# A fp32 hybrid encoder step: gated tiles stored from the gate's tile, and five pieces of work moved in the order

## The chip, the cores and the metric

One core of one Trainium2 chip. The metric is the device time of one execution in microseconds (us), taken as the median of the runs. Five engines work side by side: TensorE (PE) multiplies, VectorE (DVE), ScalarE (ACT) and GpSimd (POOL) work element by element, and SyncE (SP) issues loads and stores. POOL can issue transfers too, among them one that adds what it loads to what is already there. Each engine runs its instructions in a fixed order and waits where an operand or a buffer isn't ready yet.

## The reference, cut to what matters

One step of a two-layer streaming encoder, width 2048, over 512 new frames of one stream and 64 frames of another: 576 columns, which the kernel treats as two halves of 288. Everything is fp32.

```python
h = rmsnorm(x, g0)                                   # layer 0: gated linear attention
q, k, v, r, a1 = split(h @ w_in)
loga = log_sigmoid(a1 @ w_a2 + b_a) / 16             # per head: decay, summed over time
o = recurrence(q, k, v, loga, state)                 # 4 heads, key 256, value 512
o = o * rsqrt(mean(o * o) + eps) * g_norm
x = x + (o * silu(r)) @ w_out
h = rmsnorm(x, g1)                                   # layer 1: convolution module
a, ga, z = split(h @ w_in1 + b_in)
c = depthwise_conv31(a * sigmoid(ga), state) + b
c = silu(layernorm(c)) * silu(z)
y = rmsnorm(x + c @ w_out1, g_final)
```

## The kernel before

**Matmuls.** Each fp32 product is made of three: high part by high part (L225), high by low (L228), low by high (L231; in the stages with sums of blocks all three are on L394). Weights come in chunks of 512 KB. For each chunk SP loads `raw` (L117), ACT copies it to the high part `whi` (L125), and the low part `wlo` comes either from a DVE subtraction (L127) or, for the chunk numbers in `dma_lo` (L605), from an ACT copy with the sign turned (L129) and an adding transfer that POOL issues (L130). There are two `raw` buffers and four of `whi` and `wlo`. In the sum stages `raw` blocks are also subtracted from each other (L185), and sums of the activations are made and split (L1107, L1108, L1116 to L1119).

**Stages**, in us from the span's start. To 62: x is loaded, its squares are summed for the norm (ACT L690, POOL and DVE L691, last sum L712), the gate's low-rank product psA (L702) and the first group of q run on TensorE; the second gate weight `wa2r` is split into `w2s` by two DVE casts and a subtraction (L728 to L730) and stored to `w2d`, from where each head loads it later. To 440: the projections. 440 to 700: the heads. 700 to 930: the output projection of layer 0. 930 to 1500: the input projection of the convolution module, with the depthwise convolution on DVE, POOL and ACT; the layer norm's centring (L1313), squares (L691, L1319), mean square on TensorE (m_c L540, from ACT's high part ssch L544 and DVE's low part) and inverse root (L562 to L566) lie at 1360 to 1402, and `finish` (DVE L1324, ACT L1325, POOL L1326) then gates each of the 16 channel blocks. 1500 to 1690: the output projection, whose first pair of blocks takes the seven-product form.

**Heads.** For head h the program issues: attention, gates of head h-1 (`rblk`), decay of head h+1 (`decay`), `output(h)`, scores, states, norm. `output` writes the 512 prompt columns (ACT L974) and the 64 sample columns (DVE copy L981) of four value tiles into `ob`, of which there is one buffer (`big`). `rblk` multiplies each value tile by its gate on POOL (L1022), in place in `ob`, and SP stores it to `spill` (L1024). `decay` forms pz on TensorE (L861, L863), takes ACT functions of it (L865 to L867), and sums it over time on DVE: L868, ten scans (L873), small terms (L880 to L889) and L895; the k and q tiles are then scaled by it (L903). Temporary tiles of 128 x 576, gates, squares and loads among them, share a ring of six (`s2`, made by `tmp`).

**Order.** A scheduler orders each engine's instructions from the program's order and its own estimates; `tc.high_priority` lets an instruction pass others, and `tc.issue_after(x)` keeps it behind x in that order.

Of the kernel before, what the change touches and what calls it, by code (L numbers as in the profile page):

```python
# [17 lines left out]
P = 128  # L18
# [31 lines left out]
def emit(nc, tc, x, wg, wa1, wa2, wgo, wc, wco, par, s0, y, sp_out, ss_out, cv_out):  # L50
# [127 lines left out]
    def plan_full(w1, w2, ra):  # L178


        d = {}

        def diff(out, a, b):
            with tc.high_priority(offset=PRIO):
                nc.vector.tensor_tensor(out, a, b, ALU.subtract)  # L185

        def u0(i):
            d["r1"] = load_raw(w1, 0, f"raw{i}", *wx[ra])
            to_unit(i, d["r1"])

        def u1(i):
            d["r2"] = load_raw(w2, 0, f"raw{i}")
            diff(d["r1"], d["r2"], d["r1"])
            to_unit(i, d["r1"])

        def u2(i):
            d["r3"] = load_raw(w2, 1, f"raw{i}", *wx["r3"])
            diff(d["r2"], d["r3"], d["r2"])
            diff(d["r1"], d["r3"], d["r1"])
            to_unit(i, d["r1"])  # L200

        def u4(i):
            d["r4"] = load_raw(w1, 1, f"raw{i}")
            to_unit(i, d["r4"])

        def u5(i):
            diff(d["r1"], d["r4"], d["r1"])
            to_unit(i, d["r1"])

        chunks.extend([u0, u1, u2, lambda i: to_unit(i, d["r2"]), u4, u5,  # L210
                       lambda i: to_unit(i, d["r3"])])

# [9 lines left out]
    def mm_k(ps, hi, lo, kk, k):  # L222
        st, sp = k == 0, k == KT - 1
        for j in range(2):
            nc.tensor.matmul(ps[j], hi[:, kk, :], ah[k][:, j * HT : (j + 1) * HT],  # L225
                             start=st, stop=False)
        for j in range(2):
            nc.tensor.matmul(ps[j], hi[:, kk, :], al[k][:, j * HT : (j + 1) * HT],  # L228
                             start=False, stop=False)
        for j in range(2):  # L230
            nc.tensor.matmul(ps[j], lo[:, kk, :], ah[k][:, j * HT : (j + 1) * HT],  # L231
                             start=False, stop=sp)

    def mm_chunk(ps, ci, half):
        hi, lo = ready.pop(ci)
# [366 lines left out]
    base_c = len(chunks)  # L602
    plan(conv_groups, lambda b: wc[b])
    base_co = len(chunks)
    dma_lo.update(range(4, base_p), range(base_l + 3, base_o + 4), range(base_c + 4, base_co + 4))  # L605
    plan([[0, 1]], lambda f: wco[f])
    for f in range(2, 14, 2):
        plan_full(wco[f], wco[f + 1], ("rb", "ra")[f // 2 % 2])
# [100 lines left out]
    for k in range(KT):  # L709
        with tc.issue_after(split15) if k >= SQ_EARLY else nullcontext():  # L710
            add_sq(sqs[k // 8], xk(k)[:, 0, :], k % 8 == 0, f"x{k}", nc.gpsimd if k < 8 else nc.vector)
    nc.vector.tensor_tensor(ssq, ssq, sqs[1], ALU.add)  # L712
    a3f = s2.tile([96, T], F32, tag="s2", name="a3f")
    a3 = page(10, [96, T], "a3s", F32R)
    for j in range(2):
# [9 lines left out]
        nc.sync.dma_start(wa2r, wa2)  # L725
        nc.sync.dma_start(pr[:, PC_A:], par[:, PC_A:])
    w2 = page(9, [96, 1024], "w2s", F32R)
    nc.vector.tensor_copy(w2[:64], wa2r[:64])  # L728
    nc.vector.tensor_copy(w2[64:], wa2r[64:])
    nc.vector.tensor_tensor(w2[64:], wa2r[64:], w2[64:].bitcast(F32), ALU.subtract)  # L730
    nc.sync.dma_start(w2d, w2.bitcast(F32))

    rstd0 = rstd_from([parts(ssq, "ssx")], float(D), "x")
# [118 lines left out]
    def decay(h):  # L852
        d = hd[h]
        a3, w2 = d["aw"]
        c2 = gp.tile([P, 2, T], F32, tag="qk", name=f"c2_{h}", bufs=3)
        eq = gp.tile([P, 2, T], F32, tag="qk", name=f"eq{h}", bufs=3)
        for dt in range(2):
            f = 2 * h + dt
            for j in range(2):
                pz = px.tile([P, 512], F32, tag="ms", bufs=2, name=f"pz{f}_{j}")  # L860
                nc.tensor.matmul(pz[:, :HT], w2[:96, dt * P : (dt + 1) * P], a3[:96, j * HT : (j + 1) * HT],  # L861
                                 start=True, stop=True)
                nc.vector.tensor_scalar(eq[:, dt, j * HT : (j + 1) * HT], pz[:, :HT], col(PC_BA, f), -1.0,  # L863
                                        ALU.add, ALU.mult)
        nc.scalar.activation(c2, eq, AF.Abs)  # L865
        nc.scalar.activation(c2, c2, AF.Exp, scale=-1.0)
        nc.scalar.activation(c2, c2, AF.Ln, bias=1.0)  # L867
        nc.vector.scalar_tensor_tensor(eq, eq, 0.0, c2, ALU.max, ALU.add)  # L868
        for dt in range(2):
            for i in range(5):  # L870
                n = P if i < 4 else TS
                ts = slice(i * P, i * P + n)
                nc.vector.tensor_tensor_scan(c2[:, dt, ts], ones[:, :n], eq[:, dt, ts], 0.0, ALU.mult, ALU.add)  # L873
        sm = gp.tile([P, 2, 13], F32, tag="sm", name=f"sm{h}")
        ke = gp.tile([P, 2, 11], F32, tag="ke", name=f"ke{h}", bufs=2)
        km, ee = ke[:, :, :5], ke[:, :, 5:]
        r = sm[:, :, 0:4]
        tt = sm[:, :, 4:8]
        m = sm[:, :, 8:13]
        nc.vector.tensor_copy(r, c2[:, :, 63:TP:P])  # L880
        nc.vector.tensor_copy(tt, c2[:, :, 127:TP:P])
        for i in (2, 1, 0):
            nc.vector.tensor_tensor(tt[:, :, i : i + 1], tt[:, :, i : i + 1], tt[:, :, i + 1 : i + 2], ALU.add)
        nc.vector.tensor_tensor(m[:, :, 0:4], r, tt, ALU.subtract)
        nc.vector.tensor_scalar(m[:, :, 4:5], c2[:, :, T - 1 : T], -1.0, None, ALU.mult)
        nc.scalar.activation(km, m, AF.Exp, scale=1.0 / GN)
        o = 0
        for i in range(3):
            nc.vector.tensor_tensor(ee[:, :, o : o + 3 - i], m[:, :, i + 1 : 4],  # L889
                                    m[:, :, i : i + 1].broadcast_to([P, 2, 3 - i]), ALU.subtract)  # L890
            o += 3 - i
        nc.scalar.activation(ee, ee, AF.Exp, scale=-1.0 / GN)
        for dt in range(2):
            cv = c2[:, dt, :TP].rearrange("p (i t) -> p i t", i=4)
            nc.vector.tensor_tensor(cv, cv, r[:, dt, :].unsqueeze(2).broadcast_to([P, 4, P]), ALU.subtract)  # L895
        nc.scalar.activation(eq, c2, AF.Exp, scale=-1.0 / GN)
        nc.scalar.activation(c2, c2, AF.Exp, scale=1.0 / GN)
        d.update(eq=eq, ek=c2, km=km, ee=ee)
# [60 lines left out]
    def output(h):  # L959
# [7 lines left out]
        for vt in range(4):  # L967
            vc = slice(vt * P, vt * P + P)
            po = px.tile([P, 512], F32, tag="main", bufs=2, name=f"po{h}{vt}")
            for i in range(4):  # L970
                for n, (a, b) in enumerate(pairs):
                    nc.tensor.matmul(po[:, i * P : TP], a[:, i, vc], b[:, OFFS[i] : OFFS[i] + TP - i * P],  # L972
                                     start=(i == 0 and n == 0), stop=(i == 3 and n == 2), skip_group_check=True)
            nc.scalar.activation(ob[:, vt, :TP], po, AF.Copy)  # L974
            po = px.tile([P, 512], F32, tag="ms", bufs=2, name=f"pq{h}{vt}")
            for dt in range(2):
                nc.tensor.matmul(po[:, :TS], s0t[:, dt, vt * P : (vt + 1) * P], q[:, dt, :],
                                 start=(dt == 0), stop=False)
            for n, (a, b) in enumerate(pairs):
                nc.tensor.matmul(po[:, :TS], a[:TS, 4, vc], b[:TS, 1280:1344], start=False, stop=(n == 2))  # L980
            nc.vector.tensor_copy(ob[:, vt, TP:T], po[:, :TS])  # L981
            add_sq(sq, ob[:, vt, :], vt == 0, f"o{h}{vt}")
        d.update(o=ob, sq=sq)

    def norm(h):
        ob, sq = hd[h]["o"], hd[h]["sq"]
# [27 lines left out]
    def rblk(h, vt, ps=None):  # L1014
        if ps is None:
            t = load(blk(h, "r", vt))
        else:
            t = tmp(f"r{h}{vt}")
            with tc.high_priority(offset=PRIO):
                evac_copy(ps, t, AF.Silu)  # L1020
        ob = hd[h]["o"]
        (nc.vector if h == 3 else nc.gpsimd).tensor_tensor(ob[:, vt, :], ob[:, vt, :], t, ALU.mult)  # L1022
        if h < 3:
            nc.sync.dma_start(spill[4 * h + vt], ob[:, vt, :])  # L1024

    def start_head(h):
        hd[h] = {"aw": [tmp(f"{n}_{h}", dt=F32R) for n in ("a3", "w2")]}
# [32 lines left out]
    rot["heads"] = True  # L1060
    start_head(0)
    decay(0)
    scores(0)
    tile(0)
    values(0)
    for h in range(H):
# [7 lines left out]
        if h == 0:  # L1074
            tile(1)
        tile(2 * h + 2, scored)
        output(h)
        if h < 3:
            scores(h + 1)
        states(h)  # L1080
        if h < 3:
# [28 lines left out]
    def u_sums(h, pages, late=2):  # L1110
# [9 lines left out]
        for (n, src), i in zip((("S2", a11), ("S3", a21), ("S4", s4)), pages):  # L1120
# [4 lines left out]
                t = (t[:, 0], t[:, 1])  # L1125
            put(t, src)
            sums8[n].append(t)

    def slots_s1(h):
        for k in range(2 * h, 2 * h + 2):  # L1130
# [129 lines left out]
    def conv_evac(b, ps):  # L1260
# [23 lines left out]
        else:  # L1284
# [4 lines left out]
            if b == cin[cin.index(15) + 3]:  # L1289
                with tc.issue_after(ins):  # L1290
                    centre(2, 16)
                squares()
            elif b == cin[cin.index(15) + 4]:
                with tc.issue_after(ins):
                    ln["rs"] = rstd_from([ln["sq"]], float(D), "c")
                for g in sorted(zt):
                    finish(g)
            elif "rs" in ln:
                with tc.issue_after(ins):
                    finish(f)  # L1300
# [21 lines left out]
    def finish(f):  # L1322
# [17 lines left out]
    sums8.update((n, []) for n in ("S2", "S3", "S4"))  # L1340
    us.clear()
    us.update((2 * i, cb[i]) for i in range(8))
    run_groups(conv_groups[-1:], conv_evac, base_co - 4,
               {(0, 1): lambda: slots_u(0, 8), (1, 0): lambda: u_sums(0, ("e2", "e3", "e0")),
                (1, 1): lambda: u_sums(1, ("c0", "c4", "e1"))})
    slots_u(8, 16)
    ssq2 = stat.tile([P, T], F32, tag="ssq", name="ssq2")

# [141 lines left out]
```

## Time and profile before

| | us |
|---|---|
| runs | 1725.06, 1731.71, 1732.08 |
| median | 1731.71 |
| profiled execution | 1726.6 |
| its span | 1724.9 |
| TensorE busy in it | 1691.6 |
| DVE busy | 1192.2 |
| ACT busy | 920.5 |
| POOL busy | 496.6 |

The profile is of one execution on the one core; its times count from the start of the span. "Granted clock" (PEclk) is the share of TensorE's full speed in a stretch: 0.5 is 1.2 GHz, 1.0 is 2.4 GHz. A timeline row gives start, length, engine, line, operation, output and inputs, how many instructions the row holds, and in brackets the idle time before it and what ended that.

### The profile page before, as it was taken

The page shows a single profiled execution, that of the slowest core. Times are in us where ns is not written, and L with a number is a line of the kernel's source. Part 1 is how long each engine was busy: PE and PEld are TensorE (multiplying, and loading weights), DVE is VectorE, ACT ScalarE, POOL GpSimd, SP SyncE. Part 2 cuts the span into 40 slices and gives each one's busy share as a digit, 9 for nine tenths or more (in the row PEclk, how much of TensorE's full clock was granted, in tenths as well). Part 3 has the DMA queues.
Part 4 walks back from the last instruction along what each step waited for, and adds up shares of the span by engine and source line. Part 5 has one row for each costly group of instructions (what it writes and reads, how often), then busy time and mean ns, then how long its engine had stood idle before and what let it go on. Part 6 is the DMA issues. An engine that isn't in the chain of part 4 may idle for free.

```text
span 1724.9 us, 30811 instructions
## 1 busy us (share of the span) xinstructions
PE 1691.6 (98%) x12450; PEld 1668.8 (97%) x12450; DVE 1192.2 (69%) x1649; ACT 920.5 (53%) x1250; POOL 496.6 (29%) x452
## 2 busy tenths in 40 slices
PE   9999999999999989999999999999999999999997
PEld 8999999999999979999999999999999999999996
DVE  7686777766544551887786888878888751288775
ACT  7653344344656654744456655655555574564442
POOL 3100000000123423022223455545465442223330
PEclk9999999999999999999999999999999999999999
DMA  7963555433869766844458777777778768845464
GB/s 240 252 153 117 153 153 143 133 118 110 273 158 272 217 199 196 238 150 145 148 186 196 165 166 163 167 166 163 165 164 178 156 135 177 192 89 168 152 206 169
DMA packets 117455, 297.15 MB, mean 172 GB/s; under 512 B 11424, under 2 KB 41504, under 8 KB 116288
## 3 DMA queue, kind: packets, MB, share of 16 engines
q1 hardware_dynamic: 95472, 214.72, 41.1%
q0 software_dynamic: 21840, 80.46, 23.7%
q8 instruction: 98, 1.61, 0.4%
q14 instruction: 45, 0.37, 0.1%
HBM read 253.55 MB, written 41.57 MB: 171 GB/s over the span
## 4 chain that ended last, share of the span: by engine, by line
PE 84%; DVE 6%; DMA 4%; issue 2%; POOL 2%; ACT 1%; SPq 0%; DVEq 0%; POOLq 0%; ACTq 0%
PE ps L225 16%; PE ps L228 16%; PE ps L231 16%; PE d L394 16%; PE eS L394 6%; PE eA L394 3%; PE db L394 3%; PE pS L1003 2%; PE es L394 2%; PE psl L394 1%; PE po L972 1%; DVE wlo L127 1%; DVE c L1313 1%; DVE raw L185 1%; DMA xr<-x 1%
## 5 line engine op out<-in xcount | busy, mean ns | idle before, releaser
L125 ACT ACTIVATE whi<-raw 128x1024 fp32r<-128x1024 f32 x337 | 356.5, 1059 | 526.1 <-PE ps L228 187.6
L228 PE MATMUL ps<-h1l,whi 128*128 128x288 f32 x1536 | 330.0, 296 | 0.0
L231 PE MATMUL ps<-h1h,wlo 128*128 128x288 f32 x1536 | 329.6, 296 | 0.0
L225 PE MATMUL ps<-h1h,whi 128*128 128x288 f32 x1536 | 329.5, 296 | 0.0
L127 DVE TENSOR_TENSOR wlo<-raw,whi 128x1024 fp32r<-128x1024 f32 x204 | 253.3, 1244 | 95.9 <-ACT whi L125 94.9
L1247 DVE SCALAR_TENSOR_TENSOR acc<-ux,pr,acc 128x606 f32<-128x606 f32 x352 | 297.7, 852 | 11.8 <-ACT acc L1237 2.2
L228 PEld LDWEIGHTS ps<-h1l,whi 128*128 128x128 f32 x1536 | 248.2, 189 | 0.0
L231 PEld LDWEIGHTS ps<-h1h,wlo 128*128 128x128 f32 x1536 | 248.1, 189 | 0.0
L225 PEld LDWEIGHTS ps<-h1h,whi 128*128 128x128 f32 x1536 | 248.1, 189 | 0.0
L1245 POOL TENSOR_TENSOR sd<-sd,sd 128x606 f32<-128x606 f32 x96 | 153.0, 1594 | 72.8 <-ACT sd L1241 71.3
L185 DVE TENSOR_TENSOR raw<-raw,raw 128x1024 f32<-128x1024 f32 x108 | 146.4, 1356 | 7.5 <-DMA raw<-wg 6.4
L130 POOL DMA_DIRECT2D wlo<-wc x92 | 80.9, 879 | 214.6 <-ACT wlo L129 155.5
L129 ACT ACTIVATE wlo<-raw 128x1024 fp32r<-128x1024 f32 x133 | 138.7, 1043 | 0.0
L394 PE MATMUL d<-nh,whi 128*128 128x288 f32 x448 | 132.6, 296 | 0.0
L394 PE MATMUL d<-nh,wlo 128*128 128x288 f32 x448 | 131.9, 294 | 0.0
L394 PE MATMUL d<-nl,whi 128*128 128x288 f32 x448 | 131.8, 294 | 0.0
L691 POOL TENSOR_TENSOR ssq<-ssq,sq_x 128x576 f32<-128x576 f32 x35 | 64.4, 1839 | 191.0 <-ACT sq_x L690 184.7
L1241 ACT ACTIVATE sd<-ux,pr 128x606 f32<-128x606 f32 x112 | 87.3, 793 | 55.8 <-POOL sd L1245 55.8
L225 PE MATMUL ps<-nh,whi 128*128 128x288 f32 x480 | 107.6, 301 | 0.0
L228 PE MATMUL ps<-nl,whi 128*128 128x288 f32 x480 | 105.6, 299 | 0.0
L231 PE MATMUL ps<-nh,wlo 128*128 128x288 f32 x480 | 105.4, 298 | 0.0
L1029 POOL DMA_DIRECT2D a<-a3d x4 | 2.4, 596 | 333.8 <-DMA raw<-wg 332.2
(360 smaller groups left out, 3787.8 us busy)
## 6 DMA issues: line engine op xcount, KB each, us to landing
raw<-wc SPq DMA_DIRECT2D x96, 512.0 KB, 5.0
raw<-wg SPq DMA_DIRECT2D x94, 512.0 KB, 4.6
wlo<-wc POOLq DMA_DIRECT2D x92, 512.0 KB, 7.7
wlo<-wg POOLq DMA_DIRECT2D x33, 512.0 KB, 8.6
raw<-wgo SPq DMA_DIRECT2D x32, 512.0 KB, 4.7
raw<-wco SPq DMA_DIRECT2D x32, 512.0 KB, 4.6
ld<-pd SPq DMA_DIRECT2D x29, 288.0 KB, 8.3
vd<-v SPq DMA_DIRECT2D x32, 256.0 KB, 4.5
```

What stands on the lines that cost most here:

```text
L125: nc.scalar.activation(hi[:, :w, :], raw, AF.Copy)
L127: nc.vector.tensor_tensor(lo[:, :w, :], raw, hi[:, :w, :].bitcast(F32), ALU.subtract)
L129: nc.scalar.activation(lo, raw, AF.Copy, scale=-1.0)
L130: nc.gpsimd.dma_start(lo, src, accum_op=ALU.add)
L185: nc.vector.tensor_tensor(out, a, b, ALU.subtract)
L225: nc.tensor.matmul(ps[j], hi[:, kk, :], ah[k][:, j * HT : (j + 1) * HT], start=st, stop=False)
L228: nc.tensor.matmul(ps[j], hi[:, kk, :], al[k][:, j * HT : (j + 1) * HT], start=False, stop=False)
L231: nc.tensor.matmul(ps[j], lo[:, kk, :], ah[k][:, j * HT : (j + 1) * HT], start=False, stop=sp)
L394: nc.tensor.matmul(dst, w[:, k, :], v, start=first and k == 0 and i == 0, stop=k == 7 and i == 2, skip_group_check=True)
L1241: nc.scalar.activation(t, u[:, w : w + CW], AF.Copy, scale=cw(w))
L1245: nc.gpsimd.tensor_tensor(side, side, t, ALU.add)
L1247: nc.vector.scalar_tensor_tensor(a, v3(u[:, w : w + CW]), cw(w), a, ALU.mult, ALU.add)
```

## The change

Six edits:

1. The two casts and the subtraction of `w2s` are kept behind the last sum of squares of x (`summed`).
2. For heads 0 to 2 the gated tile is written into the gate's own temporary tile and stored from there, not in place in `ob`.
3. `decay` is cut in two; its sums (`decay_sums`) are kept behind the last sample copy of `output` (`copied`).
4. The inverse root of the convolution's layer norm is formed two blocks of matmuls later, and behind the last matmul issued before it.
5. The first of the sums for the output projection's first pair (`u_sums`) is formed before the last group of the input projection, with its results in spare tiles.
6. One more chunk of output-projection weights gets its low part by the adding transfer.

```diff
         def u0(i):
             d["r1"] = load_raw(w1, 0, f"raw{i}", *wx[ra])
-            to_unit(i, d["r1"])
+            to_unit(i, d["r1"], src=w1[:, :8, :] if i in dma_lo else None)
...
-            nc.tensor.matmul(ps[j], lo[:, kk, :], ah[k][:, j * HT : (j + 1) * HT],
-                             start=False, stop=sp)
+            state["mm"] = nc.tensor.matmul(ps[j], lo[:, kk, :], ah[k][:, j * HT : (j + 1) * HT],
+                                           start=False, stop=sp).ins
...
-    dma_lo.update(range(4, base_p), range(base_l + 3, base_o + 4), range(base_c + 4, base_co + 4))
+    dma_lo.update(range(4, base_p), range(base_l + 3, base_o + 4), range(base_c + 4, base_co + 5))
...
-    nc.vector.tensor_tensor(ssq, ssq, sqs[1], ALU.add)
+    summed = nc.vector.tensor_tensor(ssq, ssq, sqs[1], ALU.add).ins
...
-    nc.vector.tensor_copy(w2[:64], wa2r[:64])
-    nc.vector.tensor_copy(w2[64:], wa2r[64:])
-    nc.vector.tensor_tensor(w2[64:], wa2r[64:], w2[64:].bitcast(F32), ALU.subtract)
+    with tc.issue_after(summed):
+        nc.vector.tensor_copy(w2[:64], wa2r[:64])
+        nc.vector.tensor_copy(w2[64:], wa2r[64:])
+        nc.vector.tensor_tensor(w2[64:], wa2r[64:], w2[64:].bitcast(F32), ALU.subtract)
...
+        d.update(eq=eq, c2=c2)
+
+    def decay_sums(h):
+        d = hd[h]
+        eq, c2 = d["eq"], d["c2"]
         nc.vector.scalar_tensor_tensor(eq, eq, 0.0, c2, ALU.max, ALU.add)
...
-            nc.vector.tensor_copy(ob[:, vt, TP:T], po[:, :TS])
+            ins = nc.vector.tensor_copy(ob[:, vt, TP:T], po[:, :TS]).ins
...
+        return ins
...
-        ob = hd[h]["o"]
-        (nc.vector if h == 3 else nc.gpsimd).tensor_tensor(ob[:, vt, :], ob[:, vt, :], t, ALU.mult)
+        o = hd[h]["o"][:, vt, :]
         if h < 3:
-            nc.sync.dma_start(spill[4 * h + vt], ob[:, vt, :])
+            nc.gpsimd.tensor_tensor(t, o, t, ALU.mult)
+            nc.sync.dma_start(spill[4 * h + vt], t)
+        else:
+            nc.vector.tensor_tensor(o, o, t, ALU.mult)
...
-        output(h)
+        copied = output(h)
         if h < 3:
+            with tc.issue_after(copied):
+                decay_sums(h + 1)
             scores(h + 1)
...
+    def u_sums_apart(h, pages, scratch):
+
+        v, w = us[2 * h], us[8 + 2 * h]
+        a11, a12, a21, a22 = v[:, :, :HT], w[:, :, :HT], v[:, :, HT:], w[:, :, HT:]
+        S1[h], s4 = (tmp(f"{n}_{h}").rearrange("p (k t) -> p k t", k=2) for n in ("s1", "s4"))
+        t = page2(scratch, [P, 2, 2, HT], f"us_{h}")
+        s2, s3 = t[:, 0], t[:, 1]
+        sub = nc.vector.tensor_tensor
+        sub(S1[h], a21, a22, ALU.add)
+        sub(s3, a11, a21, ALU.subtract)
+        sub(s2, S1[h], a11, ALU.subtract)
+        sub(s4, a12, s2, ALU.subtract)
+        for n, src, i in zip(("S2", "S3", "S4"), (s2, s3, s4), pages):
+            t = page2(i, [P, 2, 2, HT], f"u{n}_{h}", F32R)
+            put((t[:, 0], t[:, 1]), src)
+            sums8[n].append((t[:, 0], t[:, 1]))
...
-            elif b == cin[cin.index(15) + 4]:
-                with tc.issue_after(ins):
+            elif b == cin[cin.index(15) + 6]:
+                with tc.issue_after(ins), tc.issue_after(state["mm"]):
                     ln["rs"] = rstd_from([ln["sq"]], float(D), "c")
...
+    u_sums_apart(0, ("e2", "e3", "e0"), "e1")
     run_groups(conv_groups[-1:], conv_evac, base_co - 4,
-               {(0, 1): lambda: slots_u(0, 8), (1, 0): lambda: u_sums(0, ("e2", "e3", "e0")),
-                (1, 1): lambda: u_sums(1, ("c0", "c4", "e1"))})
+               {(0, 1): lambda: slots_u(0, 8), (1, 1): lambda: u_sums(1, ("c0", "c4", "e1"))})
```

DVE's order in the first stage (`ssq0b` is the sum of squares, `w2s` the split gate weight, `wlo_138` and `wlo_144` the low parts of chunks 2 and 3), before with - and now with +:

```order
 L691 TENSOR_TENSOR ssq0b<-ssq0b,sq_x_540 128x576
-L728 CAST w2s<-wa2r 64x1024
-L729 CAST w2s<-wa2r 32x1024
 L127 TENSOR_TENSOR wlo_138<-raw_135,whi_137 128x1024
 L691 TENSOR_TENSOR ssq0b<-ssq0b,sq_x_543 128x576
-L730 TENSOR_TENSOR w2s<-wa2r,w2s 32x1024
 L127 TENSOR_TENSOR wlo_144<-raw_141,whi_143 128x1024
...
 L712 TENSOR_TENSOR ssq_168<-ssq_168,ssq0b 128x576
+L729 CAST w2s<-wa2r 64x1024
+L730 CAST w2s<-wa2r 32x1024
+L731 TENSOR_TENSOR w2s<-wa2r,w2s 32x1024
```

The three instructions stood ahead of the two low parts and now stand behind the last sum of squares.

DVE's order in head 1 (`o` is the output buffer, `pq` the sample rows in PSUM, `eq` and `c_2` the decay of head 2), before:

```order
L981 COPY o_6046<-pq_6062 128x64
L981 COPY o_6046<-pq_6084 128x64
L868 SCALAR_TENSOR_TENSOR eq_5881<-eq_5881,c_2_5880 128x1152
L873 SCALAR_TENSOR_TENSOR c_2_5880<-onesr,eq_5881 128x128 x4
L873 SCALAR_TENSOR_TENSOR c_2_5880<-onesr,eq_5881 128x64
L873 SCALAR_TENSOR_TENSOR c_2_5880<-onesr,eq_5881 128x128 x4
L873 SCALAR_TENSOR_TENSOR c_2_5880<-onesr,eq_5881 128x64
L981 COPY o_6046<-pq_6108 128x64
```

and now, the copies being on L987, the sum's first step on L874 and the scans on L879:

```order
L987 COPY o_6017<-pq_6033 128x64
L987 COPY o_6017<-pq_6055 128x64
L987 COPY o_6017<-pq_6079 128x64
L987 COPY o_6017<-pq_6103 128x64
L874 SCALAR_TENSOR_TENSOR eq_5881<-eq_5881,c_2_5880 128x1152
L879 SCALAR_TENSOR_TENSOR c_2_5880<-onesr,eq_5881 128x128 x4
```

The third and fourth copies stood behind the scans and now stand ahead of them. In head 0 all four stood behind the scans.

TensorE's order at the layer norm (`m_c` is the mean square, of the sums' high part `ssch` and low part `sscl`; `ps` are blocks of the input projection), before:

```order
L231 MATMUL ps_0_0_15120<-h1h_9787,wlo_14979 128x288
L540 MATMUL m_c<-ssch,onesr 128x288
L231 MATMUL ps_0_1_15121<-h1h_9787,wlo_14979 128x288
L225 MATMUL ps_0_0_15120<-h1h_9791,whi_14978 128x288
```

and now:

```order
L231 MATMUL ps_0_1_15207<-h1h_9791,wlo_15095 128x288
L540 MATMUL m_c<-ssch,onesr 128x288
L540 MATMUL m_c<-sscl,onesr 128x288
L225 MATMUL ps_0_0_15358<-h1h_9541,whi_15149 128x288
```

The first m_c product is number 9378 of TensorE's order before and number 9481 now: 103 matmuls later.

## Rows read from the trace of the kernel before

**Rows 1.** The page, part 1: busy time, share of the span and instructions by engine.

```profile
PE 1691.6 (98%) x12450; PEld 1668.8 (97%) x12450; DVE 1192.2 (69%) x1649; ACT 920.5 (53%) x1250; POOL 496.6 (29%) x452
```

**Rows 2.** TensorE's waits: tile and line, what it waited for, total us, times, longest.

```profile
PE pq L977 <- DVE o L981: 4.8, 1, 4.8
PE m_c L540 <- ACT ssch L544: 4.0, 1, 4.0
PE eA L394 <- DVE wlo L127: 2.2, 2, 1.3
PE pS L1003 <- DVE o L981: 2.1, 1, 2.1
PE ps L231 <- DMA wlo<-wg: 1.8, 1, 1.8
PE ps L231 <- DVE wlo L127: 1.7, 1, 1.7
```

**Rows 3.** Four slices of 25 us: busy by engine, granted clock, DMA share, GB/s.

```profile
25.00:50.00 25.00, 21.52 (x155) 21.05 (x154) 15.08 (x14) 13.94 (x20) 9.22 (x7) 0.96 0.61 158
...
600.00:625.00 25.00, 20.16 (x106) 17.82 (x106) 10.73 (x29) 14.57 (x20) 6.87 (x8) 0.86 0.58 167
1375.00:1400.00 25.00, 20.99 (x147) 20.76 (x146) 15.98 (x21) 17.36 (x21) 7.69 (x6) 0.93 0.59 123
...
1550.00:1575.00 25.00, 21.75 (x158) 20.82 (x157) 22.12 (x29) 12.21 (x17) 5.72 (x4) 1.00 0.50 156
```

**Rows 4.** DVE's timeline in the first stage.

```profile
27.77 1.44 DVE L728 CAST w2s<-wa2r 64x1024 fp32r<-64x1024 f32 x1 [0.40 <-DMA wa2r<-wa]
29.22 1.83 DVE L729 CAST w2s<-wa2r 32x1024 fp32r<-32x1024 f32 x1
31.08 2.33 DVE L127 TENSOR_TENSOR wlo<-raw,whi 128x1024 fp32r<-128x1024 f32 x1
...
35.35 1.23 DVE L127 TENSOR_TENSOR wlo<-raw,whi 128x1024 fp32r<-128x1024 f32 x1
...
52.94 0.76 DVE L545 TENSOR_TENSOR ssxl<-ssq,ssxh 128x576 fp32r<-128x576 f32 x1 [11.38 <-ACT ssxh L544]
```

**Rows 5.** Chunk 4 in the first stage, timelines of SP (the load) and ACT (the copies).

```profile
33.43 0.33 SPq L117 DMA_DIRECT2D raw<-wg  x1
...
37.10 1.06 ACT L125 ACTIVATE whi<-raw 128x1024 fp32r<-128x1024 f32 x1 [2.31 <-DMA raw<-wg]
...
39.02 0.68 ACT L716 ACTIVATE a3f<-psA 96x288 f32<-96x288 f32 x2
```

**Rows 6.** The chain of waits: transfers in it, as start, length and what is moved.

```profile
39.43 8.27 DMA wlo<-wg
...
542.50 2.52 DMA spill<-o
...
602.12 8.49 DMA spill<-o
```

**Rows 7.** DVE's timeline in heads 0 and 1: decay sums, sample copies, first use.

```profile
493.73 1.36 DVE L868 SCALAR_TENSOR_TENSOR eq<-eq,c 128x1152 f32<-128x1152 f32 x1 [4.92 <-ACT c L867]
...
504.66 0.22 DVE L981 COPY o<-pq 128x64 f32<-128x64 f32 x1 [2.73 <-PE pq L980]
...
510.49 0.75 DVE L903 SCALAR_TENSOR_TENSOR c<-ld,c 128x576 f32<-128x576 f32 x1
...
523.14 1.69 DVE L933 TENSOR_TENSOR qs<-eq,ke 128x384 f32<-128x384 f32 x4
...
556.97 4.11 DVE L873 TENSOR_TENSOR_SCAN c<-onesr,eq 128x128 f32<-128x128 f32 x10
```

**Rows 8.** ACT's timeline at the layer norm.

```profile
1388.96 0.68 ACT L544 ACTIVATE ssch<-csq 128x576 fp32r<-128x576 f32 x1 [1.98 <-DVE csq L1319]
```

**Rows 9.** Timelines of DVE, POOL and TensorE ahead of the output projection.

```profile
1504.11 4.78 DVE L682 TENSOR_TENSOR ul<-c,uh 128x576 fp32r<-128x576 f32 x7 [7.37 <-ACT uh L681]
...
1526.89 8.14 POOL L1326 TENSOR_TENSOR c<-z,c 128x576 f32<-128x576 f32 x1 [0.34 <-ACT c L1325]
...
1546.58 0.29 PE L394 MATMUL eA<-uh,wlo 128*128 128x288 f32 x1
```

More of the change, by code (lines that the diff above doesn't have):

```diff
@@ L1062, in emit @@
     decay(0)
+    decay_sums(0)
     scores(0)
```

## Prediction, written before the changed kernel was timed

> **What bounds the kernel.** I read the page's busy times first: TensorE is busy 1691.6 of 1724.9 us [rows 1], so no other engine's load matters, only where TensorE stops. Its waits, the second view, name six that the edits touch [rows 2]: 1.7 and 1.8 us in the first stage, 2.1 and 4.8 in the heads, 4.0 at the layer norm, 2.2 in the output projection's first pair, 16.6 together. The third view, slices of the span [rows 3], adds what the waits don't show: after three of these places TensorE runs part of a slice at half clock. A mean granted clock of 0.86 over 25 us is 25 x 0.14 = 3.5 us of lost work; 0.93 is 1.75, 0.96 is 1.0. TensorE has no other slack, so a wait removed is gained if nothing else is late at the same place. The timelines and the chain then say what is late next.
>
> **First stage (edit 1).** DVE does the casts at 27.77 and 29.22 and only then chunk 2's low part [rows 4], for which TensorE waits 1.7 us [rows 2]. The three instructions cost 1.44 + 1.83 and, as a pass of 1024 elements like the 1.23 of the next low part, about 1.2 more: 4.5 us. Behind the last sum of squares they lie in 11.38 us in which DVE waits for ACT [rows 4], so their new place costs nothing; without that cover it would be the 4.5. The low part can start 3.3 us earlier, and the 1.7 goes. The 1.8 is next. Chunk 4's load is issued when that low part frees its buffer (33.43), ACT copies it at 37.10 [rows 5], and the adding transfer takes 39.43 to 47.70 [rows 6]; TensorE waits for its end. The load comes 3.3 us earlier. But in the new order ACT's two copies a3f, today at 39.02 and 0.34 us each [rows 5], come ahead of chunk 4's, and they need a buffer that DVE's sums free. I estimate that the transfer is issued 2.1 us earlier. TensorE arrives 1.7 earlier, so a wait of about 1.4 to 1.8 stays: the gain is the transfer's shift, **2.1**. Bounds: 0 (the transfer keeps its time) and 4.5 (1.7 + 1.8 + 1.0 of clock). I take 2.1, being set by the transfer and not by DVE. The store of w2d, now behind three loads on SP's queue, is read only in the heads: nothing.
>
> **Heads (edits 2 and 3).** In head 2 DVE's copy into `ob` waits for the last store of gated tiles, issued at 602.12 and landed 8.49 us later [rows 6]; TensorE waits 4.8 us for the copy and then runs slow, 3.5 us of work [rows 2, 3]. After the change the copy needs only POOL's product, which ended at 602.1, when the store was issued. The store landed at 610.6 and TensorE had waited 4.8 by about then, so it got there at some 606: a margin of 4 us, and 8.3 gained. In head 1 the third sample copy stands behind the scans (4.11 us [rows 7]), and TensorE waits 2.1 [rows 2]; with the copies first this goes. What is now late: the sums themselves. In head 0 they move from 493.73 behind the copy at 504.66, 11.2 us later. From L868 to the last scaling took 510.49 + 0.75 - 493.73 = 17.5 us with the waits for operands in it, so it ends by 522.4 at worst; DVE's first use of it is at 523.14 [rows 7]. That is hidden, with under a microsecond in the worst case. The gated tiles now occupy a temporary buffer until the store has landed, and POOL does the last product before a mask that it did first: I charge 0.4, between nothing and the 8.5 us of a store for each head (a rival below). Sum 8.3 + 2.1 - 0.4 = **10.0**.
>
> **Layer norm (edit 4).** TensorE waits 4.0 us for ACT's high part, done at 1388.96 + 0.68 [rows 2, 8], and loses 1.75 to the clock [rows 3]. The product moves 103 matmuls down its order. The 288-column matmuls run at about 25 us / 190 = 0.13 us, so it comes 13.6 us later, 9 us after its operand is ready. The gating of the channel blocks starts as much later; its work lies in 100 us in which it feeds nothing on TensorE until the output projection. Gain 4.0 + 1.75 = **5.8**; below it could be 4.0, if the clock drops anyway.
>
> **First pair of the output projection (edits 5 and 6).** From 1550 to 1575 TensorE is busy 21.75 of 25 us, with DVE at 22.12 [rows 3]: DVE is late there, and the low parts are its part of it (2.2 us [rows 2]). Four sums and three splits, seven passes at 4.78 / 7 = 0.68 us, 4.8 us in all, move to before 1504, where DVE idles 7.37 us [rows 9]; one low part of 1.2 us goes to ACT and POOL. DVE is then some 6 us ahead, more than any single wait. The new adding transfer stands on POOL behind a gating product that took 8.14 us and ended at 1535.03 [rows 9]; with 8.27 us like the one in the first stage [rows 6] it lands at 1543.3, and TensorE's first product with it is at 1546.58 [rows 9]: 3 us in hand. Its extra ACT copy (1.0 us) meets an engine that is half idle. Of the 3.25 us lost in the slice I take **3.0**; bounds 0 (the transfer is late by as much) and 3.25.
>
> **Sum.** 2.1 + 10.0 + 5.8 + 3.0 = 20.9 us. Off the profiled execution, 1726.6, that is 1705.7; off the median of the runs, 1731.71, it is 1710.8. The profiled one stands 5.1 below the median, inside the runs' own spread, and I go between the two: **1708**.
>
> **The rivals.**
>
> *Waits move and the clock stays low.* A transfer of 8 us or a mask on POOL takes the place of each wait removed; the slow stretches stay. Then the first stage gives 0, the heads 4.8 + 2.1 = 6.9 less 0.4, the layer norm 4.0, the last part half, 1.5: 12.0 us, about 1717 by the same middle. For it: every edit has a next wait within 1 to 4 us by the working above. Against: the layer norm and head 2 have 9 and 4 us of margin.
>
> *The casts hold up chunk 4's transfer.* They move to where POOL issues it. If POOL could not prepare a transfer while DVE casts, it would come up to 1.44 + 1.83 = 3.3 us later, the first stage would lose 1.2 instead of gaining 2.1, and the total would be 1711. Against: a cast of 1024 elements takes 1.44 us where a two-input pass of 1024 takes 1.23 [rows 4], so it doesn't run in a faster way. The Trainium skill, "SBUF — State Buffer", section "Who interferes with whom", says that copies and casts can run in modes that take both port pairs, and that GpSimd is shut out for the whole instruction; by that rule this rival holds only if these casts run in such a mode, and their time in the trace speaks against it.
>
> *The temporary ring runs dry: slower.* Each gated tile keeps its buffer until its store has landed, 2.52 us in one head and 8.49 in another [rows 6], where the buffer was free when the product was done. Squares of the output and loads of k use the same ring of six; TensorE's next work hangs on both. It decides when a landing outlasts the time between the product and the next user of that buffer. If heads 0 to 2 each waited a whole store with the slow stretch behind it, 8.5 + 3.5 = 12 us, the heads would cost 36 instead of the 10.4 they cost now: -25.6 against 10.9 gained elsewhere, 14.7 slower, about 1744. Against: four stores go out spread over 6 us, and only the last landed late.
>
> *The change doesn't act:* the scheduler could have kept the old sequence. The orders shown say that it didn't for edits 1, 3 and 4; what is left is that each of these waits was a matter of that one execution. No change, 1729.
>
> **How the numbers follow.** About 8.7 us, 0.5%, is what a measurement here can tell from no change; that is below 1723. Forecast 0.60, moved waits 0.20, casts 0.08, no action 0.08, dry ring 0.04. The first three are faster but for a small part of the second: faster 0.86, same 0.10, slower 0.04. The range begins at 1700, where every bound is taken (4.5 + 10.4 + 5.8 + 3.25 = 24 us off 1726.6, some 1702.6, and a little of the runs' spread), and ends at 1721, past the moved waits counted off the median (1731.7 - 12 = 1719.7); the last two cases are left out.
>
> **What would show it.** Right: TensorE's waits no longer list pq and pS behind the sample copies, nor m_c behind ssch; the granted clock is 1.0 at 600 to 625 and 1375 to 1400; chunk 4's adding transfer lands near 45.6 and a wait for it of 1 to 2 us is left; TensorE is busy nearly all of the slice that answers to 1550 to 1575. Wrong: new waits in the heads on ACT's squares, on loads of k or on POOL's masks; a wait for an adding transfer before the first pair; a wait at attention 1 for DVE's scaling; or a saving in one place that comes back as a wait in the next.

## The result and the profile after

The changed kernel took 1705.16 us as a median of four runs (1702.87 to 1708.28), the kernel before 1731.09 in the same comparison: a ratio of 0.9859, 95% interval 0.9831 to 0.9887. The forecast was 1708, in the range 1700 to 1721. The profiled execution has a span of 1701.2 us against 1724.9: 23.7 us less, where the sum in the prediction was 20.9.

To see where, I took the start of the same matmul, by its number in TensorE's trace, in both profiled executions. Where the difference grows, time was gained; where the order itself changed by a few rows, the median over 30 matmuls evens it out. The times in the first column are those of the changed kernel.

| place | before minus after, us | gained there | predicted |
|---|---|---|---|
| end of the first stage, 70 us | 2.4 | 2.4 | 2.1 |
| start of the output projection, 720 us | 12.1 | 9.7 | 10.0 |
| ahead of the layer norm, 1350 us | 12.7 | 0.6 | 0 |
| behind it, 1450 us | 19.4 | 6.7 | 5.8 |
| behind the first output pair, 1600 us | 23.7 | 4.3 | 3.0 |

Some 2.6 us of the 23.7 are not waits. At three places (30 to 45, 680 to 735 and 1350 to 1385 us) the kernel before started a matmul every 133.3 ns and the changed kernel every 130.0, both without a wait: 0.4, 1.3 and 0.9 us. A slice of 25 us at the second place, before and after, with the number of matmuls in brackets:

```profile
690.00:715.00 25.00, 25.00 (x190) 25.00 (x189) 18.31 (x27) 17.68 (x26) 2.92 (x4) 1.00 0.99 286
```

```profile
690.00:715.00 25.00, 25.00 (x195) 25.00 (x194) 20.35 (x30) 21.46 (x33) 3.43 (x4) 1.00 0.91 256
```

Of the changed kernel's three profiles, the later two show 133.3 from 1350 to 1385, so this isn't shown to come from the edits.

TensorE's waits in the changed kernel; the columns are those of [rows 2]:

```profile
PE ps L231 <- DMA wlo<-wg: 1.7, 1, 1.7
PE pa L933 <- issue: 1.4, 1, 1.4
PE m_x L540 <- ACT ssxh L544: 1.3, 1, 1.3
...
PE pq L986 <- POOL athi L912: 0.8, 1, 0.8
```

Of the six waits in [rows 2] only that for chunk 4's adding transfer is left, 1.7 where it was 1.8. Two are new: 1.3 in the first stage and 0.8 in head 2, for the mask that POOL now does behind its last product. The slices that answer to [rows 3]:

```profile
25.00:50.00 25.00, 22.89 (x174) 22.43 (x172) 15.58 (x14) 15.08 (x22) 10.50 (x7) 1.00 0.66 176
...
600.00:625.00 25.00, 25.00 (x154) 22.21 (x154) 13.74 (x35) 17.62 (x23) 8.60 (x9) 1.00 0.71 210
1375.00:1400.00 25.00, 25.00 (x192) 25.00 (x191) 9.72 (x16) 18.47 (x20) 5.43 (x6) 1.00 0.87 191
...
1550.00:1575.00 25.00, 25.00 (x191) 25.00 (x190) 19.73 (x21) 12.54 (x16) 8.81 (x6) 1.00 0.49 162
```

The granted clock is 1.00 in all four; TensorE is busy through the three later ones.

### The profile page after: what moved, and what is told of

The parts are those of the page before. It is cut to its first block, busy times and chain, and to the rows that moved or that the text cites. A ratio compares the mean times of both kernels' runs of the same rounds, so it can differ in the third digit from the quotient of the medians.

```text
span 1701.2 us, 30804 instructions
## 1 busy us (share of the span) xinstructions
PE 1681.0 (99%) x12450; PEld 1660.4 (98%) x12450; DVE 1193.8 (70%) x1648; ACT 921.6 (54%) x1251; POOL 490.8 (29%) x453
## 4 chain that ended last, share of the span: by engine, by line
PE 95%; DMA 2%; ACT 1%; DVE 1%; issue 0%; POOL 0%; SPq 0%; DVEq 0%; POOLq 0%; ACTq 0%
PE ps L225 17%; PE ps L231 17%; PE ps L228 17%; PE d L394 16%; PE eS L394 10%; PE eA L394 5%; PE db L394 3%; PE es L394 2%; PE pS L1010 2%; PE po L978 2%; PE psl L394 1%; DMA raw<-wg 1%; PE pa L943 1%; ACT xh L674 1%; PE pa L933 1%; DMA ld<-pd 0%
```

## The experiments

The theory: each edit takes away the wait that the prediction names, at its own place, so undoing one gives that back and leaves the rest. The rivals differ from edit to edit. There are twelve runs. Eight of them (edits 1 to 6 undone, the casts without POOL's additions, and the changed kernel once more) are one execution each, so I read the loss at the edit's place, by the same matmuls, and not the total. A loss is against the changed kernel's first profile where nothing else is said.

**Edit 1 undone** (the three instructions without `issue_after(summed)`).

```diff
-    with tc.issue_after(summed):
-        nc.vector.tensor_copy(w2[:64], wa2r[:64])
+    nc.vector.tensor_copy(w2[:64], wa2r[:64])
```

> The changed kernel with edit 1 undone: the casts and the subtraction of the gate weight stand ahead of chunk 2's low part again; all else as changed. If each place keeps its own account, the span grows by about 2.5 us (1701 to 1704), all of it before 60 us: TensorE waits 1.7 us for chunk 2's low part again, the adding transfer of chunk 4 lands near 47.7 instead of 45.3, and the half-clock stretch behind it comes back. Rival: the adding transfers alone set the stage, so that the wait moves but the sum stays; then under 0.5 us. On the casts: 0.68 us each in the new place, 1.44 and 1.83 in the old one beside POOL's additions; if POOL's company is the cause they take 1.4 to 1.9 again here, if the operands are they stay at 0.7.

TensorE waited 1.7 us for chunk 2's low part again and went on behind chunk 4's transfer at 47.02 and not at 45.33. From 25 to 60 us it lost 2.1, so the wait is what the edit takes away. But the granted clock stayed at 1.00 from 25 to 50 us: the half-clock stretch of the profile before didn't come back with the same waits. (Another 1.3 us went between 70 and 125 us, where matmuls started every 133.3 ns instead of 130.0 at a clock shown as 1.00; the changed kernel did that, too, in a later run, so it isn't shown to be the edit's.) DVE's timeline:

```profile
27.73 0.87 DVE L728 CAST w2s<-wa2r 64x1024 fp32r<-64x1024 f32 x1 [0.97 <-DMA wa2r<-wa]
28.61 1.83 DVE L729 CAST w2s<-wa2r 32x1024 fp32r<-32x1024 f32 x1
30.48 2.32 DVE L127 TENSOR_TENSOR wlo<-raw,whi 128x1024 fp32r<-128x1024 f32 x1
```

and that of the changed kernel, where the casts stand behind POOL's additions:

```profile
27.33 2.46 DVE L127 TENSOR_TENSOR wlo<-raw,whi 128x1024 fp32r<-128x1024 f32 x1
...
38.97 0.68 DVE L729 CAST w2s<-wa2r 64x1024 fp32r<-64x1024 f32 x1
39.66 0.68 DVE L730 CAST w2s<-wa2r 32x1024 fp32r<-32x1024 f32 x1
```

**Casts early, POOL's additions left out.** The same edit, and for the squares 1 to 7 of x only ACT's squaring: this kernel leaves out half of the norm's sum.

```diff
-            add_sq(sqs[k // 8], xk(k)[:, 0, :], k % 8 == 0, f"x{k}", nc.gpsimd if k < 8 else nc.vector)
+            if 0 < k < 8:
+                nc.scalar.activation(tmp(f"sq_x{k}"), xk(k)[:, 0, :], AF.Square)
+            else:
+                add_sq(sqs[k // 8], xk(k)[:, 0, :], k % 8 == 0, f"x{k}", nc.vector)
```

> Edit 1 undone as in the first look, and POOL's seven additions of squares of x left out (so half of the first norm's sum is left out; ACT still squares). It asks what made the casts 0.9 to 1.8 us and chunk 2's low part 2.3. If it was POOL's additions beside them, both casts take 0.7, the low part 1.2, and TensorE's wait of 1.7 us for it is gone or under 0.5 although the casts stand ahead of it. If it is the cast's own length and shape, the casts stay at 0.9 to 1.8 and the wait at 1 or more.

```profile
28.02 0.69 DVE L731 CAST w2s<-wa2r 64x1024 fp32r<-64x1024 f32 x1 [0.66 <-DMA wa2r<-wa]
28.72 0.68 DVE L732 CAST w2s<-wa2r 32x1024 fp32r<-32x1024 f32 x1
...
31.48 1.23 DVE L127 TENSOR_TENSOR wlo<-raw,whi 128x1024 fp32r<-128x1024 f32 x1
```

The operands are the same and the casts take 0.7, the low part 1.23: POOL's additions were the cause. The wait fell only to 1.1, since DVE's order here put an addition and the subtraction ahead of the low part as well. TensorE's wait for chunk 4's transfer was 3.5: its load, with the store of w2d now issued just ahead of it, landed after 5.1 us where it had taken 3.7 [rows 5].

**Edit 2 undone.**

```diff
-            nc.gpsimd.tensor_tensor(t, o, t, ALU.mult)
-            nc.sync.dma_start(spill[4 * h + vt], t)
+            nc.gpsimd.tensor_tensor(o, o, t, ALU.mult)
+            nc.sync.dma_start(spill[4 * h + vt], o)
```

> The changed kernel with edit 2 undone: the gated tiles of heads 0 to 2 are written in place in the output buffer and stored from there; the order of TensorE, DVE and ACT is unchanged. If the landing of the last store is what the next head's output waits for, head 2 loses about 7.5 us again (a wait of some 5 on the first copies and the half-clock stretch), the sum 1708 to 1709, and heads 0 and 1 nothing. Rival: with the four copies ahead of the decay sums the wait is mostly gone without edit 2; then under 3 us. Second rival: the ring of temporary tiles pays for edit 2 elsewhere; then some wait on squares or loads is shorter here than in the changed kernel.

Head 2 lost 4.8 us more than in the changed kernel, which itself waits 0.9 for the mask there; 7.5 had been expected. Heads 0 and 1 lost nothing, but for the load below. The wait was 2.4, on ACT's first copy, and the granted clock from 600 to 625 was 0.86 again, 3.5 us. The wait is shorter than the 4.8 of [rows 2] because the store took 5.60 us here and 8.49 in [rows 6]; from the chain of this run:

```profile
602.09 5.60 DMA spill<-o
607.86 0.60 ACT o L980
608.51 2.52 PE po L978 x12
```

Who waited for transfers to or from `spill`, first in this run, then in the changed kernel (engine, tile and line, us in total, times), and last a row of SP's own waits in the changed kernel:

```profile
DVE o L987: 18.0, 2
ACT o L980: 7.7, 2
ACT uh L681: 5.1, 2
```

```profile
ACT uh L681: 5.0, 2
```

```profile
SPq L848 <- DMA spill<-ld: 4.2, 1, 4.2
```

In the changed kernel the slowest store, the last one of head 1's tiles, lands 8.8 us after its issue. Of the engines that compute only ACT waits, behind the heads (L681), and it also does without the edit. SP's queue does wait for that store: one of the four loads of k and q for head 3 (L848) needs the temporary buffer and stands 4.2 us, and 1.3 and 1.0 us in the changed kernel's two later profiles. So the wait that the rival of the temporary ring names is there. But all four loads had landed by 613.7, DVE's first scaling with them began at 617.65, and TensorE lost nothing: from 620 to 665 us the time gained on the kernel before stays at 11.1.

**Edit 3 undone** (`decay_sums(h + 1)` right behind `decay(h + 1)`, no `issue_after`).

```diff
             decay(h + 1)
+            decay_sums(h + 1)
...
-            with tc.issue_after(copied):
-                decay_sums(h + 1)
```

> The changed kernel with edit 3 undone: the decay sums may stand ahead of the sample copies again. If the copies behind the scans were the wait, head 1 loses about 2.3 us and head 2 nothing or little (its buffer is free now, so its copies stand behind the scans, too: up to 4 us more if TensorE reaches them while the scans run). Rival: the later sums cost something in head 0, where the changed kernel lost 0.7 us between 440 and 530; then those 0.7 come back here and the sum changes by 1.6 only.

```profile
PE pS L1010 <- DVE o L987: 2.7, 2, 2.1
```

Head 1 lost 3.9 us (530 to 575): the wait, 2.24 by the starts of the matmuls, and a clock of 0.93 behind it, 1.75. Head 2 waited 0.8 at the same place. From 480 to 530, head 0, the difference to the changed kernel moved by 0.3: the sums 11 us later cost nothing there that this can show. From 530 to 665 it came to 3.5, the mask's wait of 0.9 not being there; behind 680 matmuls started every 133.3 ns here and every 130.0 in the changed kernel, which isn't the wait's.

**Edit 4 undone** (`+ 6` back to `+ 4`, and no `issue_after(state["mm"])`).

```diff
-            elif b == cin[cin.index(15) + 6]:
-                with tc.issue_after(ins), tc.issue_after(state["mm"]):
+            elif b == cin[cin.index(15) + 4]:
+                with tc.issue_after(ins):
```

> The changed kernel with edit 4 undone: the mean square of the convolution's layer norm two blocks earlier and without the last matmul ahead of it. If the wait for the squares and the slow stretch behind it were all, the span grows by 6.2 to 6.7 us (1707.5 to 1708), at 1385 minus 13 on this kernel's clock, and TensorE waits 4 us for ACT's high part. Rival: part of that gain belongs to another edit (the squares come later or earlier by the work before them); then the wait is not 4 us but 2 or less, or the clock stays at 1.0 and the loss is 4.

```profile
PE m_c L540 <- ACT ssch L544: 4.6, 1, 4.6
```

```profile
1375.00:1400.00 25.00, 20.41 (x137) 20.18 (x136) 16.08 (x19) 17.86 (x21) 9.21 (x8) 0.86 0.62 132
```

From 1350 to 1500 it lost 7.3 us: a wait of 4.6 and a half-clock stretch twice as long as in [rows 3], 3.5 by the mean clock. The two add up to 8.1; some of the half-clock stretch probably lay inside the wait and cost nothing.

**The changed kernel again** (no edit), on the chip of the runs with edits 5 and 6 undone.

> The changed kernel itself once more, on the chip of this call, to set the undone versions against. The four looks so far lost 2.7 to 3.9 us at the first attention product near 467 us, where the first profile of the changed kernel lost 1.6, and no edit differs there. If that is a weight load that lands later on some chips or in some executions, and not the undone edit, this run shows it too: a loss of 1.5 to 4 at 467 behind a load of 6 to 9 us. If it belongs to the undone edits, this run shows 1.6 again.

The loss at the first attention product was 1.06 here, 3.9 in the run with edit 2 undone. That product needs DVE's scalings, these need ACT's exponentials of the decay, and in ACT's queue the exponentials stand behind the high part of a weight chunk. The chunk's load on SP, its high part, and the table load with which the exponentials begin, first with edit 2 undone, then here:

```profile
445.56 0.91 SPq L117 DMA_DIRECT2D raw<-wg  x1
...
462.59 1.07 ACT L125 ACTIVATE whi<-raw 128x1024 fp32r<-128x1024 f32 x1 [6.29 <-PE ps L228]
...
465.21 1.28 ACT L902 ACT_TABLE_LOAD   x1
```

```profile
448.41 0.51 SPq L117 DMA_DIRECT2D raw<-wg  x1
...
461.42 1.06 ACT L125 ACTIVATE whi<-raw 128x1024 fp32r<-128x1024 f32 x1 [3.04 <-DMA raw<-wg]
...
464.42 1.28 ACT L902 ACT_TABLE_LOAD   x1 [0.39 <-DVE sm L889]
```

The load landed 16.9 us after its issue there (at 462.50; the matmul in brackets ended 0.1 us later) and 12.9 here; 12.8 in the kernel before, where the loss was 1.07, and 14.4 in the changed kernel's first profile, where it was 1.55. The expectation's 6 to 9 us seem to be those of the next chunk's load, which SP issued some 8 us later. In the eight profiled executions that lost more than 1.1 the attention product started 7.8 us after that ACT row, so TensorE pays for a late landing. In the other six the exponentials waited for DVE's sums, as in the last row here, and the loss was 1.06 or 1.07. The changed kernel's three profiles lost 1.55, 1.06 and 3.7, so this is one source of the spread of its runs; and it lost over 2.5 with each of edits 1, 2, 3, 4 and 6 undone, so none of these makes it.

**Edit 5 undone, edit 6 undone**, against that run on the same chip. `u_sums(0, ...)` back in the group's table; `base_co + 5` back to `base_co + 4`.

```diff
-    u_sums_apart(0, ("e2", "e3", "e0"), "e1")
...
+               {(0, 1): lambda: slots_u(0, 8), (1, 0): lambda: u_sums(0, ("e2", "e3", "e0")),
```

> The changed kernel with edit 5 undone: the four sums and three splits of the output projection's first pair are formed inside the last group of the input projection again; edit 6 stays. If DVE's lateness was the wait and the seven passes are most of the work moved (4.8 of 6 us), 3 to 4 us of the 4.3 gained between 1548 and 1580 are lost again, with TensorE waiting on low parts and sums. Rival: the one low part taken off DVE (edit 6) was enough; then under 1.5.

```diff
-    dma_lo.update(range(4, base_p), range(base_l + 3, base_o + 4), range(base_c + 4, base_co + 5))
+    dma_lo.update(range(4, base_p), range(base_l + 3, base_o + 4), range(base_c + 4, base_co + 4))
```

> The changed kernel with edit 6 undone: that one chunk's low part by DVE again; edit 5 stays. If edit 5 put DVE some 5 us ahead, 1.2 us more of DVE work cost 0 to 0.7 us. Rival: both were needed, and each undone loses most of the 4.3; then over 2.5.

From 1500 to 1600 the first lost 1.9 us, the second 1.15, of the 4.3 gained by both. Both expectations missed: neither edit has most of it, and neither is free. The 1.3 us left over seem to go only where both are undone; no run undoes these two alone.

**What is left in the first stage.** Three versions of the changed kernel, timed in rounds beside it.

> The changed kernel once more, timed in rounds on the chip of this call, as the measure for the three that follow. 1702 to 1709 us, 0.985 to 0.988 of the kernel before.

```diff
-    dma_lo.update(range(4, base_p), range(base_l + 3, base_o + 4), range(base_c + 4, base_co + 5))
+    dma_lo.update(range(5, base_p), range(base_l + 3, base_o + 4), range(base_c + 4, base_co + 5))
```

> The changed kernel with chunk 4's low part by DVE, which stands idle from 42 to 50 us, in place of ACT's signed copy and the adding transfer. The wait of 1.5 to 2 us for that transfer goes. If the next thing late is ACT's high part of the sum of squares, which stands in ACT's queue behind chunk 7's high part and so behind a load that lands near 49, TensorE arrives there as much earlier and waits 3.2 us in place of 1.4: the sum is the same within 0.5 us. Rival: the transfers are the stage's limit and with one less the load lands earlier, too; then 1.5 to 3 us are gained.

The next one adds to this, with `ssx` being ACT's high part of the sum of squares:

```diff
-        with tc.high_priority(offset=PRIO):
+        with tc.high_priority(offset=PRIO), tc.issue_after(state["ssx"]) if i == 7 else nullcontext():
             nc.scalar.activation(hi[:, :w, :], raw, AF.Copy)
```

> As the run before, and chunk 7's high part on ACT is kept behind the high part of the sum of squares. If those two waits are all that the first stage has left, both go: 3 us less than the changed kernel, TensorE without a loss over 0.5 us between 12 and 60 us. Rival: what is behind comes late in turn (chunk 7's low part, or the copies of q); then under 1.5 us.

and the last one does the same for chunk `base_l + 5`, behind the second exponential of head 0's decay.

> As the run before, and in head 0 one weight chunk's high part on ACT is kept behind the two exponentials of the decay. ACT stood 3 to 6 us at that chunk's load with the exponentials queued behind it, and TensorE lost 1.1 to 3.9 us at the first attention product. If that queue is the cause the loss is under 0.6 us in this run whatever the load takes, another 1 to 3 us less than the run before. Rival: the sums on DVE or the loads of k are as late; then the loss stays over 1.

| | median us | ratio to before, 95% | span | loss from 40 to 55 us | loss near 466 us |
|---|---|---|---|---|---|
| changed | 1706.23 | 0.9868 (0.9847 to 0.9889) | 1704.5 | 2.7 | 3.7 |
| chunk 4 by DVE | 1701.93 | 0.9848 (0.9829 to 0.9867) | 1699.3 | under 0.4 | 1.1 |
| and the sum's high part first | 1702.91 | 0.9857 (0.9837 to 0.9878) | 1700.5 | under 0.4 | 2.8 |
| and the exponentials first | 1704.37 | 0.9860 (0.9839 to 0.9880) | 1701.4 | under 0.4 | 1.1 |

With chunk 4 by DVE both waits of the first stage went, against my expectation: I thought the second would grow. As the rival said, with one adding transfer less chunk 7's load landed earlier, and ACT came to the sum's high part in time. First the changed kernel's first profile, then this run:

```profile
48.88 1.06 ACT L125 ACTIVATE whi<-raw 128x1024 fp32r<-128x1024 f32 x1 [4.37 <-DMA raw<-wg]
...
50.13 0.67 ACT L544 ACTIVATE ssxh<-ssq 128x576 fp32r<-128x576 f32 x1
```

```profile
47.37 1.06 ACT L125 ACTIVATE whi<-raw 128x1024 fp32r<-128x1024 f32 x1 [2.44 <-DMA raw<-wg]
...
48.62 0.68 ACT L544 ACTIVATE ssxh<-ssq 128x576 fp32r<-128x576 f32 x1
```

So the next version had nothing left to gain there. In the last one the exponentials no longer stand behind the load, and the loss is still 1.1: ACT now waits for DVE's sums, as the rival said.

```profile
461.25 1.28 ACT L904 ACT_TABLE_LOAD   x1 [5.25 <-DVE sm L891]
```

TensorE also waited 1.6 us more at the next head's pz for the load of w2d. The edit may still take the load's scatter out of the loss; one profile doesn't show that. By medians chunk 4 by DVE is 4 us below the changed kernel; the intervals overlap, so only its two waits are shown to be gone, not the total.

## Why the prediction was right, point by point

**First stage.** 2.4 measured, 2.1 predicted: the low part went ahead, the wait of 1.7 went, and the transfer's end moved by 2.4 (47.74 to 45.33, the starts behind it). That was partly luck: the transfer was issued 1.7 earlier and not 2.1 (37.74 for 39.43), and it happened to take 7.5 us for 8.3. Two steps were off inside that. The clock came back to 1.00, which I hadn't counted; and a wait of 1.3 for ACT's high part of the sum of squares, which I hadn't named, took most of that. The clock's part was also larger than the 1.0 that I read: the half-clock stretch of the profile before goes on behind the slice that ends at 50, 1.7 us in all.

```profile
48.00:50.00 2.00, 2.00 (x11) 2.00 (x11) 0.00 (x0) 1.46 (x2) 0.25 (x1) 0.54 0.87 184
50.00:52.00 2.00, 2.00 (x11) 2.00 (x11) 0.00 (x0) 1.02 (x2) 0.61 (x1) 0.60 0.79 190
```

Nor does the clock's part follow from the edit: with edit 1 undone it stayed at 1.00, and with edits 5 and 6 undone, where edit 1 is in place, there was a half-clock stretch near 47 us again.

"It doesn't run in a faster way" was wrong. The casts take 0.68, under the 1.23 of a two-input pass; the 1.44 and 1.83 that I argued from were taken beside POOL's additions. The Trainium skill, "SBUF — State Buffer", section "Who interferes with whom", has it: a DVE copy or cast in a two-port mode, and a DVE pass with two inputs in SBUF where the GpSimd instruction reads SBUF, contend with GpSimd for a shared port pair, and the one that comes first holds it for its whole instruction while the other is blocked. These runs agree: the cast 0.69 without POOL's additions and up to 1.83 with them, the low part 1.23 and 2.32. The rival built on it (the casts hold up chunk 4's transfer) didn't occur, but not for my reason: POOL had issued that transfer at 37.74 to 38.75, and the first cast began at 38.97. What a cast does to a transfer that is being issued wasn't shown.

**Heads.** 9.7 against 10.0, but 1.0 of the 9.7 came from the closer start of matmuls between 680 and 720 us, which nothing in the prediction had counted; the waits gave 8.7. Head 2 gave 8.3, as predicted, after it had lost 0.9 at the mask (0.4 charged); head 1 gave 2.3 (2.1); head 0 lost 0.7, 0.5 of it to the load; and 0.3 went between heads 1 and 2. That the sum for the heads came out so near is luck. The rival of the temporary ring had its mechanism right, as SP's wait of 4.2 us for a store shows, but that load had time in hand and TensorE lost nothing. That this could have been decided beforehand I doubt: nothing in the rows read before says which tile takes which buffer.

**Layer norm.** 6.7 against 5.8. The wait and the half-clock stretch gave 5.8, the undone version loses them again, and the other 0.9 is once more the start of matmuls every 130.0 ns for every 133.3.

**First pair.** 4.3 against 3.0. The term was read from 25 - 21.75 us of busy time; the four pauses between matmul starts in the trace before add up to 3.9 there, since a matmul's busy time covers a part of the gap behind it. And "more than any single wait" gave all of it to edit 5: undone alone, edit 5 costs 1.9 and edit 6 1.15.

**Total.** Without the closer starts of matmuls the profile gained some 21.1 us, and the sum was 20.9. This fits better than the parts do: the heads were 1.3 short and the first pair had 1.3 too much. The forecast of 1708 stood between the sum off the profiled execution, 1705.7, and the sum off the median, 1710.8; the measured median lies 2.8 below it, and the closer starts, which no term had counted, gave 2.6 in the profile.

## What to carry to other kernels

Where one engine is busy 98% of the span, the list of its waits and the slices with a low clock are nearly the whole of what an edit of the order can gain; add both, and look at each place for what is late next. An operation's duration is only its own if no other engine holds it up meanwhile, as POOL's additions did the casts here: before arguing from it, look what POOL and DVE do in the same microseconds. A buffer that is held until a store has landed costs that store's slowest landing, not its median; let the store leave from a tile that nobody is waiting for, and look at SP's own waits to see whether a load now stands there instead. When a row waits for a load, follow the buffers to the load that filled it: with two buffers it isn't the last one issued.

## What the runs showed of the hardware that I had not expected

The half-clock stretch doesn't follow from the waits alone: pauses of 1.9 and 1.9 us, 14 us apart, were followed by one in the kernel before (0.96 from 25 to 50) and pauses of 1.9, 1.8 and 1.1 by none with edit 1 undone; the changed kernel showed 1.00 in that slice in two profiles and 0.93 in the third, behind a pause of 2.7. A pause of 2.1 with edit 6 undone was followed by 3.4 us at half clock, one of 2.2 with edit 4 undone by none. One 512 KB load of weights, at the same place of the program, landed 12.4 to 16.9 us after its issue in the fourteen profiled executions. And matmuls of 288 columns that follow each other without a wait start every 133.3 ns through most of the input projection (950 to 1330 us) in all fourteen, but every 130.0 in a few other stretches of some of them, at the same granted clock of 1.00: from 70 to 125 us eight had 130.0 and six 133.3. The cause stays open.
